# Sums of squares of the new x: their matmuls further back in TensorE's order, their running sum in another tile

## The chip, the core and the metric

The kernel runs on one core of a Trainium2 chip. The metric is the time of one execution on the device in microseconds (us). Engines are named as in the profile: PE is TensorE's matmul side and PEld its weight loads, DVE is VectorE, ACT is ScalarE, POOL is GpSimd, SP is SyncE, whose queue issues most of the DMAs.

## What is computed

Two layers of a decoder trunk are run on 288 tokens: 256 of a prompt and 8 sequences of 4 sample tokens. Each layer has three sub-layers: a SwiGLU feed-forward, a token mixer, and another feed-forward; the mixer of the first layer ("even") is window attention beside an RG-LRU branch, that of the second ("odd") is HGRN2. Each sub-layer is wrapped as follows, and the change touches the root mean square of the new x that the next sub-layer takes:

```python
def _rms_norm(x, gain):
    xf = x.astype(jnp.float32)
    inv = lax.rsqrt(jnp.mean(xf * xf, axis=-1, keepdims=True) + EPS)
    return (xf * inv).astype(x.dtype) * gain.astype(x.dtype)
def _pre(x, c, g_pre, ada_w, ada_b):
    mod = jax.nn.silu(c) @ ada_w + ada_b
    shift, scale, gate = jnp.split(mod[:, None, :], 3, axis=-1)
    return _rms_norm(x, g_pre) * (1 + scale) + shift, gate
def _post(x, y, gate, g_post, res_w):
    return x + res_w * (1 + gate) * _rms_norm(y, g_post)
```

## The kernel before

Activations lie feature-major: x is a tile of 128 partitions by 8 blocks by 288 tokens. Six sub-layers are numbered i = 0 to 5; i = 1 is the even mixer, i = 4 the odd one. Each has an input projection (`proj_in`, PSUM tiles `pj`), its own inner work, and an output projection (`proj_out`, tiles `y`), followed in `out_proj` by the norms and by `pre`, which makes the next input `h`. Weights come as f32 (`raw`, 1 MB each, two buffers) and are split by ACT (`whi`) and DVE (`wlo`) into two halves in a matmul format that PE runs faster; one product of a 128x128 weight block is three matmuls, two with `whi` and one with `wlo` ("a step" below). A wide tile `raw` holds two halves of 1024 columns, one for each output block j.

The conditioning products (`ada`, tiles `aw`, 1 MB each, three buffers) are spread over the whole run in chunks of four matmuls (eight matmul records), and when the last chunk of a group is done, `ada_finish` copies the sums with ACT (`asb`), turns them on PE (`adaT`) and forms `mod`, `modA` or `modG` on DVE.

The order on PE and SP is the program's own order. The program writes it with a planner: `clk["t"]` is a modelled PE clock, main work is a generator (`drive`), and side work is a list of generators (`side`). A side generator that yields a number is taken up again that many modelled microseconds later; one that yields nothing, after what it issued is modelled to end. So a yield in a side generator decides how much of the main work stands ahead of the generator's next matmuls in PE's order. ACT, DVE and POOL are ordered by a list scheduler from the program order and its own estimate of when inputs are ready; PE and SP execute strictly in the order written.

`out_proj` needs, for the mean square of the next x, the mean square of the present x (`clk["xw"]`, tile `xw`). That is what `x_stats` makes: four ACT squares of two blocks of x each (tiles `xsq`), three adds, sixteen small matmul records with a constant weight (`xms`), and one DVE op into `xw`. It runs once at the start, where the adds are on DVE, and four times (i = 0 to 3) as a side generator after `pre`, where the adds are on POOL. `xw` is read only at the end of the sub-layer that follows. The tile `yss` (pool `tp`, one buffer, 3 x 288 columns) is `out_proj`'s running sum of squares of y and of the products with x; it is read last by the sums that `late` issues near the end of the output projection. The `xsq` tiles come from the pool `bp` of 27 buffers, which also holds the mixers' tiles.

In the even mixer `done` puts the first four output blocks into padded tiles `xr`; POOL fills the borders of `xr` from the carried state; `gates` makes the width-4 convolution on DVE (one TENSOR_SCALAR and three SCALAR_TENSOR_TENSOR into `xc` for each of four blocks) and two gate products on PE (`rgr`, `rgi`). POOL's queue there also holds the stores `out_k_old` and `out_v_old`, which copy the carried window from `kc` and `vc` to memory.

Of the kernel before, what the change touches and what calls it, by code (L numbers as in the profile page):

```python
# [9 lines left out]
F32 = mybir.dt.float32  # L10
# [7 lines left out]
NT = 288  # L18
# [31 lines left out]
def tile_trunk(ctx: ExitStack, tc: tile.TileContext, I: dict, O: dict):  # L50
    nc = tc.nc
    SY = nc.sync
    clk = {"t": 0.0, "dma": 0.0, "step": 0.0}
# [82 lines left out]
    tp = ctx.enter_context(tc.tile_pool(name="tp", bufs=8))  # L136
# [3 lines left out]
    def flat(name, dt=F32):  # L140
        return bp.tile([128, 2 * PW], dt, tag="b", name=name)
# [7 lines left out]
    def small(name, shape, tag=None, bufs=None):  # L149
        return sp.tile(shape, F32, tag=tag or "s%d" % int(np.prod(shape[1:])), name=name, bufs=bufs)  # L150

    def aux_ps(name):
        return ps.tile([128, 512], F32, tag="ps", name=name, bufs=8)
# [66 lines left out]
    def after(r, prior):  # L220
        tc.add_manual_dep(r.ins, prior.ins.name, NOSYNC, reason="order")
        return r
# [210 lines left out]
    def mod_of(i):  # L433
        if i not in mods:
            mods[i] = (mp.tile([128, 24, 9], F32, tag="mod", name=f"mod{i}", bufs=3),
                       mp.tile([128, 8, 9], F32, tag="modA", name=f"modA{i}", bufs=3),
                       mp.tile([128, 8, 9], F32, tag="modG", name=f"modG{i}", bufs=3))
        return mods[i]
# [10 lines left out]
    def ada_finish(i, g, acc):  # L449
        mod, mA, mG = mod_of(i)  # L450
        if clk["t"] < clk.get("hold", 0.0):
            yield clk["hold"] - clk["t"] + 0.01
        asb = flat("asb")[:, :512]
        A.activation(asb, acc, AF.Copy)
        yield [asb]
        pt = aux_ps("adaT")
        o, nj = (16, 2) if g else (0, 4)
        for b in range(4):
            if g:
                T.matmul(pt[:, 18 * b:18 * b + 18], lhsT=asb[:, 128 * b:128 * b + 128], rhs=foldg, start=True, stop=True)  # L460
            else:
                T.transpose(pt[:, 128 * b:128 * (b + 1)], asb[:, 128 * b:128 * (b + 1)], ident)
        m = 9 if g else 32
        V.tensor_tensor(
            out=mod[:, o:o + 4 * nj, :].rearrange("p (j b) m -> p b j m", b=4),
            in0=pt[:, :4 * nj * m].rearrange("p (b j m) -> p b j m", b=4, j=nj)[:, :, :, 0:9],
            in1=adab[:, 24 * i + o:24 * i + o + 4 * nj].rearrange("p (j b) -> p b j", b=4).unsqueeze(3)
            .to_broadcast([128, 4, nj, 9]),
            op=OP.add)
        V.scalar_tensor_tensor(out=mG if g else mA, in0=mod[:, 8 + 8 * g:16 + 8 * g, :], scalar=1.0,  # L470
                               in1=(gph if g else gpre)[:, 8 * i:8 * i + 8].unsqueeze(2).to_broadcast([128, 8, 9]),
                               op0=OP.add, op1=OP.mult)
# [20 lines left out]
    def ada_steps(parts):  # L493
        n = ada_st["n"]
        ada_st["n"] += 1
        i, c = chunks[n]
        ada_load_to(n)
        g = int(c >= NC0)
        if c in (0, NC0):
            ada_st["acc"] = aux_ps(f"ada{i}{g}")  # L500
        acc = ada_st["acc"]
        w = aw[n][0]
        m = 512 // parts
        for q in range(parts):
            if q:
                yield
            for j in range(4):
                k = 2 * (c - NC0) + j // 2 if g else c
                T.matmul(acc[32 * j:32 * j + 32, m * q:m * q + m], lhsT=sc[:, k, :],
                         rhs=w[:, 512 * j + m * q:512 * j + m * q + m],  # L510
                         start=c in (0, NC0) and q == 0, stop=c in (NC0 - 1, NCH - 1) and q == parts - 1)
        ada_load_to(n + AW)
        if c in (NC0 - 1, NCH - 1):
            side(ada_finish(i, g, acc))
# [42 lines left out]
    def sums(out, t, first, last, m=None):  # L557
        for j in range(4):
            T.matmul(out[32 * j:32 * j + 32, :], lhsT=mean1 if m is None else m, rhs=t[:, NG * j:NG * j + NG],
                     start=first, stop=last)  # L560
# [24 lines left out]
    def x_stats(prior=None):  # L585
        w = small("xw", [128, NG], tag="xw", bufs=2)
        clk["xw"] = w
        if prior:
            yield 12.0
        t0 = flat("xsq")[:, :2 * NT]  # L590
        for b in range(0, NB, 2):
            t = flat("xsq")[:, :2 * NT] if b else t0
            r = A.activation(t, x[:, b:b + 2, :].rearrange("p c t -> p (c t)"), AF.Square)
            if prior:
                after(r, prior)
            if b:
                (G if prior else V).tensor_tensor(out=t0, in0=t0, in1=t, op=OP.add)
        yield
        p = aux_ps("xms")[:, :NG]
        for c in range(2):  # L600
            sums(p, t0[:, NT * c:NT * c + NT], c == 0, c == 1)
        V.tensor_scalar(out=w, in0=p, scalar1=EPS, scalar2=None, op0=OP.add)
# [103 lines left out]
    def pre_first():  # L706
# [47 lines left out]
        def before(k):  # L754
            if k == 0:
                for _ in x_stats():
                    pass
                ada(0)
                warm(WARM[1])
                u = root(clk["xw"], None, "xiv")  # L760
                refine(u, clk["xw"], V)
                iv = tp.tile([128, NT], F32, tag="ivs", name="ivf", bufs=1)
                A.activation(iv, spread(u, "xivb", 99.0), AF.Copy)
                st["iv"] = iv
                table(AF.Silu)
                finish(0)
                warm(WARM[2])
                ada(1)
                warm(WARM[3])
                finish(1)  # L770
                warm(WARM[4])
            if k + 2 < NB:
                ada(k + 2)
# [19 lines left out]
    def out_proj(i, nk, hk):  # L793
# [120 lines left out]
        if i < NSUB - 2:  # L914
            side(x_stats(da.last))
# [728 lines left out]
```

## Time and profile before

| | us |
|---|---|
| three runs | 1319.61, 1322.71, 1323.49; median 1322.71 |
| the profiled execution | 1321.75 |
| its span, first to last instruction | 1320.0 |
| PE busy | 1281.6 (97%) |
| PEld / DVE / ACT / POOL busy | 1184.9 / 777.1 / 638.2 / 194.2 |
| mean granted TensorE clock | 0.989 of 2.4 GHz |

A row of the timeline gives start, duration, engine, line, operation, the tile written and the tiles read, the number of instructions merged into the row and, in square brackets, the idle time ahead of it with what ended that. The line is that of a helper everywhere, so tiles name the work. In the row of a matmul the start is what counts; ends are modelled. A row of the stretches gives from:to, length, and then the busy time of PE, PEld, DVE, ACT and POOL with instruction counts, the granted clock, the share of the DMA engines' time and GB/s.

### The profile page before, as it was taken

Reading aid. Unit: us, or ns where it says so; the run is one execution under the profiler, and the core shown is the slowest. Engines: PE = TensorE matmul, PEld = TensorE weight load, DVE = VectorE, ACT = ScalarE, POOL = GpSimd, SP = SyncE. Lnnn points to the kernel's source line nnn. Section 1 sums busy time; section 2 is a strip of 40 time slices with the busy share of each in tenths; the row PEclk is TensorE's granted clock in tenths of the full one; section 3 lists DMA queues with packets and bytes.
Section 4 is the critical chain, followed back from the end, with each engine's and each line's share of the span. In section 5 each row is a group of like instructions: output and inputs, shape, how many; then the busy total and the mean of one; then the engine's idle time right before and its main releaser. Section 6 shows DMA issues by size and latency. Waiting matters only on the chain.

```text
span 1320.0 us, 25241 instructions
## 1 busy us (share of the span) xinstructions
PE 1281.6 (97%) x10413; PEld 1184.9 (90%) x10413; DVE 777.1 (59%) x1406; ACT 638.2 (48%) x1091; POOL 194.2 (15%) x295
## 2 busy tenths in 40 slices
PE   9999999969899999999999999999999998999997
PEld 8999999957687899999799999978888988999997
DVE  6635436557846554555555555559788877555442
ACT  5434435456745544444544444464443566444442
POOL 0000001153022100011200001135344131000010
PEclk9999999989989999999999999999999999999999
DMA  9776555396256655444586454467644352555441
GB/s 366 264 313 246 203 211 205 133 373 236 96 212 236 266 205 169 159 160 160 224 323 219 160 164 171 146 263 264 228 157 164 132 192 68 192 174 174 160 160 37
DMA packets 39413, 263.48 MB, mean 200 GB/s; under 512 B 4917, under 2 KB 5493, under 8 KB 9217
## 3 DMA queue, kind: packets, MB, share of 16 engines
q1 hardware_dynamic: 35136, 249.09, 51.7%
q0 software_dynamic: 4160, 12.77, 2.8%
q8 instruction: 82, 1.34, 0.4%
q14 instruction: 35, 0.28, 0.1%
HBM read 254.69 MB, written 7.15 MB: 198 GB/s over the span
## 4 chain that ended last, share of the span: by engine, by line
PE 85%; DVE 6%; ACT 3%; DMA 2%; POOL 2%; issue 1%; DVEq 0%; POOLq 0%; ACTq 0%
PE pj L94 49%; PE y L94 24%; PE ada L94 4%; DVE wlo L94 2%; PE lv L94 1%; DMA aw<-in_w_ada 1%; PE o L94 1%; DMA kc<-in_kc 1%; PE adaT L94 1%; ACT L94 1%; POOL hv L94 1%; DMA raw<-in_wo_in 1%; PE adaf L94 1%; PE warm L94 1%; ACT whi L94 1%
## 5 line engine op out<-in xcount | busy, mean ns | idle before, releaser
L94 PE MATMUL pj<-h,whi 128*128 128x288 f32 x3552 | 723.3, 298 | 1.9 <-ACT h L94 1.8
L94 PEld LDWEIGHTS pj<-h,whi 128*128 128x128 f32 x3552 | 569.3, 188 | 35.3 <-issue 23.1
L94 DVE TENSOR_TENSOR wlo<-raw,whi 128x1024 fp32r<-128x1024 f32 x326 | 400.6, 1240 | 290.2 <-ACT whi L94 288.6
L94 PE MATMUL pj<-h,wlo 128*128 128x288 f32 x1776 | 518.2, 294 | 1.2 <-DVE wlo L94 1.2
L94 ACT ACTIVATE whi<-raw 128x1024 fp32r<-128x1024 f32 x326 | 340.4, 1057 | 350.4 <-PE pj L94 143.1
L94 PEld LDWEIGHTS pj<-h,wlo 128*128 128x128 f32 x1776 | 335.3, 189 | 2.0 <-DVE wlo L94 1.9
L94 PE MATMUL y<-mh,whi 128*128 128x288 f32 x1408 | 280.9, 295 | 0.0
L94 PEld LDWEIGHTS y<-mh,whi 128*128 128x128 f32 x1408 | 225.8, 188 | 2.1 <-issue 1.7
L94 PE MATMUL y<-mh,wlo 128*128 128x288 f32 x704 | 207.9, 295 | 0.0
L94 POOL TENSOR_TENSOR yss<-yss,ysq 128x288 f32<-128x288 f32 x55 | 59.2, 1078 | 798.5 <-ACT ysq L94 790.5
L94 PEld LDWEIGHTS y<-mh,wlo 128*128 128x128 f32 x704 | 132.4, 188 | 0.0
L94 DVE TENSOR_TENSOR fs<-fs,pj 128x288 f32<-128x288 f32 x88 | 39.5, 453 | 93.1 <-PE pj L94 92.1
L94 PE MATMUL ada<-aw,cT 128*32 128x256 f32 (+1 forms) x712 | 71.2, 499 | 3.8 <-DMA aw<-in_w_ada 3.8
L94 ACT ACTIVATE mh<-fs 128x288 fp32r<-128x288 f32 x88 | 37.8, 434 | 58.5 <-DVE fs L94 58.5
L94 ACT ACTIVATE fs<-pj 128x288 f32<-128x288 f32 x88 | 34.8, 400 | 37.2 <-PE pj L94 37.0
L94 DVE TENSOR_TENSOR mh<-fs,mh 128x288 fp32r<-128x288 f32 x88 | 39.5, 453 | 10.7 <-ACT mh L94 10.7
L94 PE MATMUL y<-o,whi 128*128 128x288 f32 x192 | 39.6, 300 | 0.0
L94 ACT ACTIVATE ysq<-y 128x288 f32<-128x288 f32 x42 | 17.0, 405 | 45.1 <-PE y L94 45.1
L94 PEld LDWEIGHTS ada<-aw,cT 128*32 128x32 f32 x712 | 17.2, 110 | 22.2 <-issue 15.5
L94 ACT ACT_TABLE_LOAD x27 | 34.6, 1283 | 5.0 <-DVE oivw L94 3.9
L94 ACT ACTIVATE h<-hv,mod,modA 128x256 fp32r<-128x256 f32 x40 | 23.7, 592 | 21.4 <-DVE hv L94 21.4
L94 DVE TENSOR_TENSOR yg<-y,modG 128x32 f32<-128x32 f32 x48 | 8.9, 186 | 41.6 <-ACT yg L94 41.6
(292 smaller groups left out, 1096.5 us busy)
## 6 DMA issues: line engine op xcount, KB each, us to landing
raw<-in_wf_in SPq DMA_DIRECT2D x88, 1024.0 KB, 5.0
aw<-in_w_ada SPq DMA_DIRECT2D x64, 1024.0 KB, 6.4
raw<-in_wf_out SPq DMA_DIRECT2D x44, 1024.0 KB, 4.9
raw<-in_wo_in SPq DMA_DIRECT2D x16, 1024.0 KB, 7.4
awf<-in_w_ada SPq DMA_DIRECT2D x8, 1024.0 KB, 9.5
raw<-in_we_in SPq DMA_DIRECT2D x7, 1024.0 KB, 7.7
raw<-in_we_out SPq DMA_DIRECT2D x4, 1024.0 KB, 7.1
S<-in_s POOLq DMA_DIRECT2D x16, 256.0 KB, 6.6
```

The costliest lines, as they stand in the source:

```text
L94: r = f(*args, **kw)
```

## The change

Three edits. In `x_stats` the running sum `t0` of the squares no longer takes a tile of `bp` but the first 576 columns of a tile with the tag `yss`. Where `x_stats` runs as a side generator, it now yields 40 modelled microseconds between the adds and the matmuls, where it yielded until the adds were modelled to end. In `ada_finish`, a generator that starts before the end of `pre` (`clk["hold"]`) waits for 3.0 modelled microseconds after that end instead of 0.01. The number of instructions on each engine is the same.

```diff
@@ -449,7 +449,7 @@
     def ada_finish(i, g, acc):
         mod, mA, mG = mod_of(i)
         if clk["t"] < clk.get("hold", 0.0):
-            yield clk["hold"] - clk["t"] + 0.01
+            yield clk["hold"] - clk["t"] + 3.0
         asb = flat("asb")[:, :512]
         A.activation(asb, acc, AF.Copy)
         yield [asb]
@@ -587,7 +587,8 @@
         clk["xw"] = w
         if prior:
             yield 12.0
-        t0 = flat("xsq")[:, :2 * NT]
+        acc = tp.tile([128, 3, NT], F32, tag="yss", name="xss", bufs=1)
+        t0 = acc.rearrange("p c t -> p (c t)")[:, :2 * NT]
         for b in range(0, NB, 2):
             t = flat("xsq")[:, :2 * NT] if b else t0
             r = A.activation(t, x[:, b:b + 2, :].rearrange("p c t -> p (c t)"), AF.Square)
@@ -595,7 +596,7 @@
                 after(r, prior)
             if b:
                 (G if prior else V).tensor_tensor(out=t0, in0=t0, in1=t, op=OP.add)
-        yield
+        yield 40.0 if prior else None
         p = aux_ps("xms")[:, :NG]
         for c in range(2):
             sums(p, t0[:, NT * c:NT * c + NT], c == 0, c == 1)
```

## Rows read from the trace of the kernel before

**Rows 1.** The page's head: the span of the profiled execution.

```profile
span 1320.0 us, 25241 instructions
```

**Rows 2.** PE's waits: waiter, releaser, total us, times, longest us.

```profile
PE xms L94 <- POOL xsq L94: 9.9, 2, 9.4
...
PE adaT L94 <- ACT asb L94: 0.6, 1, 0.6
```

**Rows 3.** Timeline of the even mixer's start: PE around the sums.

```profile
285.39 0.29 PE L94 MATMUL pj<-h,wlo 128*128 128x288 f32 x1
...
295.07 0.71 PE L94 MATMUL xms<-xsq,mean 128*32 128x72 f32 x16 [9.39 <-POOL xsq L94]
```

**Rows 4.** Stretches of 5 us around it: busy us by engine, granted clock, DMA.

```profile
285.00:290.00 5.00, 0.68 (x6) 0.44 (x4) 1.51 (x3) 1.32 (x6) 2.17 (x4) 0.67 1.02 405
290.00:295.00 5.00, 0.00 (x0) 0.00 (x0) 4.09 (x3) 1.74 (x2) 5.00 (x18) 0.50 1.01 360
295.00:300.00 5.00, 4.93 (x33) 2.82 (x33) 4.51 (x10) 0.00 (x0) 0.55 (x3) 0.50 0.49 201
300.00:305.00 5.00, 5.00 (x36) 3.79 (x33) 5.00 (x9) 2.33 (x4) 0.00 (x0) 0.96 0.77 269
```

**Rows 5.** Timeline there, POOL alone.

```profile
288.61 0.55 POOL L1040 DMA_DIRECT2D out_v_old<-vc  x1 [1.27 <-DMA vc<-in_vc]
289.18 1.41 POOL L94 TENSOR_TENSOR xsq<-xsq 128x576 f32<-128x576 f32 x1
...
290.56 0.22 POOL L94 COPY xr<-cin 128x24 f32<-128x24 f32 x1
...
293.64 1.38 POOL L94 TENSOR_TENSOR xsq<-xsq 128x576 f32<-128x576 f32 x1
```

**Rows 6.** Timeline there, DVE alone: the convolution around `xw`.

```profile
293.24 2.13 DVE L94 SCALAR_TENSOR_TENSOR xc<-xr,sm,xc 128x312 f32<-128x312 f32 x1
295.85 0.23 DVE L94 TENSOR_SCALAR xw<-xms 128x72 f32<-128x72 f32 x1 [0.49 <-PE xms L94]
296.00 1.90 DVE L94 SCALAR_TENSOR_TENSOR xc<-xr,sm,xc 128x312 f32<-128x312 f32 x4
...
304.66 0.53 DVE L94 SCALAR_TENSOR_TENSOR xc<-xr,sm,xc 128x312 f32<-128x312 f32 x1
```

**Rows 7.** Timeline there, PE behind the sums: two steps, gate products, a chunk.

```profile
303.06 0.42 PE L94 MATMUL pj<-h,whi 128*128 128x288 f32 x2
...
303.45 0.43 PE L94 MATMUL pj<-h,whi 128*128 128x288 f32 x2
...
304.26 0.69 PE L94 MATMUL rgr<-xc,rgw 128*128 128x312 f32 x2
...
307.23 0.69 PE L94 MATMUL rgr<-xc,rgw 128*128 128x312 f32 x2
...
308.28 0.69 PE L94 MATMUL rgr<-xc,rgw 128*128 128x312 f32 x2
...
309.42 1.06 PE L94 MATMUL ada<-aw,cT 128*32 128x512 f32 x8
```

**Rows 8.** Timeline at the other places: i = 2's start, then the odd mixer's.

```profile
434.98 0.66 PE L94 MATMUL adaT<-ident,asb 128*128 128x128 f32 x4 [0.65 <-ACT asb L94]
...
890.48 0.46 PE L94 MATMUL xms<-xsq,mean 128*32 128x72 f32 x16 [0.47 <-POOL xsq L94]
...
891.07 2.01 ACT L94 ACTIVATE whi<-raw 128x1024 fp32r<-128x1024 f32 x2 [1.29 <-DMA raw<-in_wo_in]
...
891.81 0.78 POOL L94 TENSOR_SCALAR K<-F 128x288 f32<-128x288 f32 x1
...
892.57 1.57 PE L94 MATMUL dg<-Q,K 128*128 128x128 f32 x11
```

**Rows 9.** Timeline of the even mixer's middle: a small product and its DVE reader.

```profile
329.05 0.75 PE L94 MATMUL rp<-rx,rot 128*128 128x288 f32 x2
...
333.61 0.45 DVE L94 TENSOR_TENSOR rx<-rp,cs 128x288 f32<-128x288 f32 x1
```

## The prediction

> **What bounds the kernel now.** I read the page first. PE is busy for 1281.6 of the 1320.0 us of the span [rows 1] and the chain of work that ended last is mostly PE, so only what shortens PE's idle time, or speeds up PE, can show. PE's waits come next: over the whole run it waits 9.9 us for the sums `xms`, in two places, and 9.4 of that in one of them; the other waits are small, among them 0.6 us of `adaT` for its copy `asb` [rows 2]. So the change can gain where the 9.4 us lie, at the start of the even mixer: PE ends a step at 285.39 + 0.29 = 285.68 and starts the sums at 295.07 [rows 3]. The stretches show the second cost: the granted clock falls to 0.50, the lower of its two levels (1.2 GHz), while PE stands, and stays there after PE is back; the mean over 300 to 305 is 0.96, so the higher level returns at about 300.4 (0.4 us of 5 at half) [rows 4].
>
> Then I ask why the sums were late. ACT's squares are early; POOL's adds are late because POOL issues four stores of the carried window first, each held by the load of its tile; the last is issued at 288.61, the first add starts at 289.18 and the last ends at 293.64 + 1.38 = 295.02 [rows 5]. Between these adds, in the same queue, stand the copies that fill the borders of `xr` (290.56) [rows 5]. That is the point of the case: the same late POOL queue also feeds DVE's convolution, and the convolution feeds PE's gate products, which stand 9 us further on in PE's order [rows 7]. What ends last once the sums are gone is DVE.
>
> **The change part by part.** *The wait in the even mixer.* With the sums moved 40 planned us back, PE goes on at 285.68 with what stood between them and the first gate product: about ten steps and two chunks. A step takes 303.45 - 303.06 = 0.39 us and a chunk 1.06 [rows 7], so some 6.0 us; with the eight transposes `adaT`, moved 3 us back, about 1 us more, PE is at the first gate product at 292.7. It cannot run it then. DVE's row of the convolution at 293.24 ends at 295.37; then `xw` waited 0.49 and took 0.23, and the next four operations ran from 296.00 to 297.90 [rows 6]. The first block of `xc` is among those. Without `xw` they start at 295.37, 0.63 us earlier, and so does everything behind them on DVE, which was busy in all of 300 to 305 and in 4.51 us of the 5 before [rows 4]. The last operation of the fourth block ended at 304.66 + 0.53 = 305.19 [rows 6] and will end at 304.56. PE's fourth pair of gate products then starts 0.05 us later (the lag from POOL's add to the sums, 295.02 to 295.07 [rows 3, 5]) and takes 309.42 - 308.28 = 1.14 us [rows 7]: the chunk behind it starts at 305.75 where it started at 309.42. So of 9.4 us of wait at most 3.7 come back here; the rest is waited for by `rgr` instead of `xms`.
>
> The clock takes part of it. PE will idle from 292.7 to about 297.3 and then in short pieces; idle from 285.68 on, it was at the lower level in all of 290 to 295 [rows 4]. If it is low at the fourth pair, that pair takes 2.28 us and ends at 306.9: 2.5 us are left. Before, the level came back 5.3 us after PE had resumed (295.07 to 300.4) [rows 3, 4]; counted from the third pair, now near 303, that is 308.3, and the 1.4 us to there lose half of it, 0.7. So the ends are 1.8 us (low throughout) and 3.7 us (full throughout). No row is nearer to one of them, PE being busy for about a quarter of 292.7 to 304 (two pairs, a small product and a step); I take the middle, 2.7.
>
> The Trainium skill ("TensorE: Matmul & The Clock Gate", section "Part 1: The HAM clock gate") says that TensorE left idle goes back to half rate and is given the full rate again only after sustained work. That speaks against this change, because it leaves an idle gap in the same place; by the rule the term would be the low end, 1.8, and by a clock that only a gap as long as the old one lowers it would be 3.7. The 0.50 at 290 to 300 agrees with the rule for the long gap; no row shows a gap of 4 to 5 us broken by short work.
>
> *The sums in their new place.* Sixteen records cost 0.46 us at full clock [rows 8]. In the even mixer they stood in a stretch that DVE will bound, so their old place gives nothing back and the new place costs 0.46, above 0 and below 0.7 (the half-clock row [rows 3]). That leaves 2.2 us for the mixer. In the feed-forwards the work is moved from one dense stretch to another: 0.
>
> *i = 2's start.* The sums did not wait there; `adaT` behind them waits 0.65 us for its copy [rows 8]. That generator starts after `hold`, so it is not moved. PE comes 0.46 us earlier; the copy does not. Bounds: -0.46 (all waited away) to +0.65 (the planner puts other steps in front); I take 0, the planner's clock being 0.5 us early there too. *The odd mixer.* 0.47 us of wait and 0.46 of sums leave this place [rows 8]. But the next side product, `dg`, needs K, whose second half POOL ends at 891.81 + 0.78 = 892.59, while `dg` starts at 892.57 and lasts 1.57 for both halves [rows 8]; PE can't be more than some tenths earlier there. Bounds 0 to 0.9; I take 0.2. *i = 3's start* has no wait [rows 2]: 0.
>
> *The 3 us in `ada_finish`.* It acts at the two mixers, where the generator starts before `hold`. Queued behind the copy `asb` on ACT are the splits `whi`; if the list scheduler puts the copy behind two splits that wait for their weights (891.07 to 893.08 in the odd mixer [rows 8]), PE's transposes wait for it. In the even mixer the wait of PE for the convolution hides that; in the odd mixer it costs up to 2.6 us. I take 0, since the copy's place in the program stays ahead of those splits, and keep -2.6.
>
> *The tile.* `yss` is last read by the sums near 257 and next written after the mixer's own output products, so it adds no wait; `bp` has one tile less in use. SP: the loads of the next `aw` tiles, queued behind chunks, go out up to 11 us earlier, into stretches whose DMA engines are full (1.02, 1.01) [rows 4]; what they could delay, the weights of output blocks 8 and 9, is needed only behind the fourth gate pair. 0.
>
> Sum: 2.7 - 0.46 + 0 + 0.2 = 2.4 us. The profiled execution took 1321.75, so 1319.35; the median of the three runs is 0.96 above it, so the forecast is 1322.71 - 2.4 = 1320.3, its own range 1317.4 (3.7 + 0.65 + 0.9 = 5.3 gained) to 1322.2 (0.5 gained).
>
> **The rivals.** *A, the wait comes back in full.* It needs DVE's convolution not to be the next bound: the list scheduler draws up DVE's and POOL's orders anew and could put the border copies ahead of the adds. For it: the largest wait in the profile, and the lower clock behind it. Against it: the copies stand behind the same four stores and DVE's queue was full from 295.9 on [rows 4 to 6]. Gain: 9.39, plus half of the 4.93 us that PE ran at 0.50 (2.47) [rows 4], plus 0.65 and 0.47 [rows 8]: 13.0, so 1309.7; a part of it gives 5 to 13. *B, nothing is left.* The 2.4 us are lost again in the mixer's second half, where DVE carries the softmax; 1322.7, give or take 1. For it: DVE's lag there; against it: all of that follows PE's output blocks in order. *C, slower.* The sums' new place lies near 328 in the even mixer, where DVE lags: `rp` started on PE at 329.05 and its reader on DVE at 333.61, 4.6 us later [rows 9]. `xw` joins that queue and holds one of the eight PSUM banks meanwhile. If PE's next output tile needs that bank, PE stands for up to 4.6 us and runs as long at the lower level behind it as it did before, 2.47: 1322.7 - 2.4 + 4.6 + 2.5 = 1327.4. It decides from the point where all other seven banks are in use within the 4.6 us. That the sums aren't moved at all is no rival: PE's order is written out by the program.
>
> **How the numbers follow.** Forecast 0.48, A (whole or in part) 0.23, B 0.19, C 0.10. 0.3% is 4.0 us, about what a measurement of this kernel can tell from no change. Faster by more: all of A and a fifth of the forecast, 0.33; slower by more: C, 0.10; the rest, 0.57, within. A alone holds more than the 0.2 that may be left out, so the range goes from 1309.5 to 1324.5 and leaves out C and the tails.
>
> **What would show it.** Right: in the changed trace `xms` waits nowhere, PE's longest wait at the even mixer's start is `rgr` for `xc`, of 4 to 6 us, the granted clock still touches 0.50 between 290 and 305, and the chunk behind the fourth gate pair starts at 305.5 to 307.5. Wrong: no PE wait over 2 us there (A); the same chunk earlier but the output projection of the mixer no earlier than 374 (B); a wait of a `pj` tile near 328 with `xw` as its releaser (C); `adaT` waiting for `asb` in the odd mixer (the 2.6 us).

## The result and the profile after

The changed kernel is slower.

| | before | after |
|---|---|---|
| median of four executions each, us | 1321.45 (1319.61 to 1323.49) | 1332.47 (1331.56 to 1334.03) |
| ratio after to before | | 1.0084, 95% interval 1.0064 to 1.0105 |
| profiled execution / its span | 1321.75 / 1320.0 | 1331.56 / 1329.8 |
| mean granted TensorE clock | 0.989 | 0.988 |

The forecast was 1320.3 with a range of 1309.5 to 1324.5, and slower by over 0.3% had the smallest chance, 0.10. The head of the page of the changed kernel answers [rows 1]:

```profile
span 1329.8 us, 25239 instructions
```

The section on the change has the number of instructions on each engine the same. On PE it is not: the pages count 10407 where the kernel before has 10413; DVE, ACT and POOL have as many as before. That is a first sign of a program drawn up anew.

The waits of PE over the whole run (waiter, releaser, total us, times, longest us) answer [rows 2]:

```profile
PE pv L94 <- ACT pTs L94: 5.7, 3, 4.1
PE rgr L94 <- issue: 5.2, 1, 5.2
PE rgr L94 <- DVE xc L94: 3.8, 2, 3.6
...
PE pT L94 <- DVE den L94: 2.2, 1, 2.2
PE adaT L94 <- ACT asb L94: 2.0, 3, 1.4
```

The 9.4 us of `xms` for POOL are gone, as the change wants. In their place PE waits for the gate products `rgr` (9.0 us together; the first of these waits has no releaser in the profile, but stands ahead of the first product that needs `xc`) and, further on, in the attention (`pv`, `pT`). PE around the gates, against [rows 3, 7]: the last step, the four `rgr`, and the chunk behind them.

```profile
292.34 0.29 PE L94 MATMUL pj<-h,wlo 128*128 128x288 f32 x1
297.79 1.38 PE L94 MATMUL rgr<-xc,rgw 128*128 128x312 f32 x2 [5.16 <-issue]
...
300.01 1.38 PE L94 MATMUL rgr<-xc,rgw 128*128 128x312 f32 x2
...
302.64 1.38 PE L94 MATMUL rgr<-xc,rgw 128*128 128x312 f32 x2 [0.22 <-DVE xc L94]
...
308.17 1.38 PE L94 MATMUL rgr<-xc,rgw 128*128 128x312 f32 x2 [3.62 <-DVE xc L94]
...
310.52 1.94 PE L94 MATMUL ada<-aw,cT 128*32 128x512 f32 x8
```

The first gate product is near where the prediction put it (297.3), the chunk behind the fourth pair 1.1 us later than before instead of 1.8 to 3.7 earlier, and nothing but gate products stands between 292.6 and 310.5. The stretches (columns as in [rows 4]) show the clock. It is still 1.00 in 290 to 295, goes to the lower level (0.50 in the stretches of 1 us) while PE waits for the first gate, and again around the fourth pair; it was 1.00 from 305 on in the kernel before (the last row).

```profile
290.00:295.00 5.00, 2.63 (x22) 2.40 (x18) 2.96 (x3) 2.00 (x2) 4.98 (x18) 1.00 1.03 399
295.00:300.00 5.00, 2.21 (x4) 1.20 (x5) 5.00 (x11) 2.82 (x4) 1.69 (x3) 0.71 1.02 425
300.00:305.00 5.00, 4.33 (x9) 2.22 (x8) 5.00 (x7) 2.50 (x5) 2.93 (x2) 0.61 0.51 213
305.00:310.00 5.00, 1.83 (x4) 1.18 (x4) 4.16 (x6) 0.52 (x2) 1.68 (x1) 0.73 0.00 0
310.00:315.00 5.00, 5.00 (x22) 2.58 (x21) 0.58 (x2) 4.39 (x8) 0.96 (x2) 0.59 0.31 72
```

```profile
305.00:310.00 5.00, 5.00 (x27) 3.21 (x25) 3.15 (x5) 4.10 (x8) 2.96 (x3) 1.00 0.37 154
```

The decisive view is none of these but the order of PE's instructions in the two programs. From `adaT` of the even mixer on (a step is one accumulating step of an output block):

```
before   adaT, 2 steps, SUMS, 3 steps, chunk, 3 steps, chunk, 4 steps,
         pair 0, pair 1, rp, 1 step, pair 2, pair 3, chunk, 7 steps, ...
changed  chunk, adaT, 3 steps, chunk, 6 steps,
         pair 0, pair 1, pair 2, pair 3, chunk, 1 step, rp, 9 steps, ...
```

Not only the sums have moved. The program draws up PE's order by a clock of its own while it issues instructions; without the sums (0.56 us on that clock) and with the later transposes, side work falls due at other steps. All four gate pairs come together, three steps earlier, and the attention's products come out in another order too. The prediction took for granted that the rest of the order only shifts. The order on ACT, DVE and POOL is drawn up from the program's order, so it can change as well; the attention below shows it on ACT.

How much each stretch lost I worked out from the stretches of 1 us: idle is the length less PE's busy time, half-clock loss is the busy time times one less the granted clock. Both together, in the even mixer: 12.1 us before and 16.3 after in 285 to 318, 0.8 and 1.9 in 318 to 345, 10.2 and 12.0 in 345 to 400. From 256 to 400 that is 24.5 and 31.8. From the end of i = 0 to the end of i = 1 (both at the product `xivb`) before took 147.67 us and the changed kernel 154.98, 7.3 more:

```profile
262.68 1.11 PE L94 MATMUL xivb<-xiv,pick 128*128 128x72 f32 x8
410.35 1.11 PE L94 MATMUL xivb<-xiv,pick 128*128 128x72 f32 x8
```

and in the changed kernel

```profile
263.26 1.11 PE L94 MATMUL xivb<-xiv,pick 128*128 128x72 f32 x8
418.24 1.11 PE L94 MATMUL xivb<-xiv,pick 128*128 128x72 f32 x8 [1.02 <-DVE xiv L94]
```

Over the whole of i = 1 the lost time is 26.9 and 35.1, 8.2 apart, so it accounts for the longer mixer within about 1 us (within some 2 us in the kernels below). The rest of the 9.8 us of span is 0.6 ahead of 263, 0.3 in i = 2 and 3 together and 1.8 in the odd mixer (222.89 and 224.65, `xivb` to `xivb`), less 0.1 behind it.

### The profile page after: what moved, and what is told of

Read it like the earlier page. It is cut to its first block, busy times and chain, and to the rows that moved or that the text cites. A ratio compares the mean times of both kernels' runs of the same rounds, so it can differ in the third digit from the quotient of the medians.

```text
span 1329.8 us, 25239 instructions
## 1 busy us (share of the span) xinstructions
PE 1286.7 (97%) x10407; PEld 1186.7 (89%) x10407; DVE 780.1 (59%) x1406; ACT 637.9 (48%) x1091; POOL 191.7 (14%) x295
## 4 chain that ended last, share of the span: by engine, by line
PE 61%; DVE 4%; ACT 3%; DMA 2%; issue 1%; POOL 1%; SPq 0%; DVEq 0%; ACTq 0%; POOLq 0%
PE pj L94 36%; PE y L94 17%; PE ada L94 2%; DVE wlo L94 2%; PE lv L94 1%; DMA S<-in_s 1%; PE o L94 1%; POOL hv L94 1%; DMA raw<-in_wo_out 1%; DVE yg L94 1%; ACT hv L94 1%; ACT whi L94 1%; DVE hv L94 0%; ACT L94 0%; DVE x L94 0%
## 5 line engine op out<-in xcount | busy, mean ns | idle before, releaser
L94 DVE TENSOR_TENSOR mh<-fs,mh 128x288 fp32r<-128x288 f32 x88 | 39.5, 452 | 10.2 <-ACT mh L94 10.2
L94 PEld LDWEIGHTS y<-o,whi 128*128 128x128 f32 x192 | 31.5, 192 | 1.9 <-ACT tab L94 0.8
```

Of the source, the lines that this page charges most:

```text
L94: r = f(*args, **kw)
```

## The experiments

Theory 1: the move of the sums is worth what was forecast, and the order drawn up anew costs (in the first kernels narrower: the order at the gates). Rivals: the later transposes hold up DVE's convolution (theory 2), or the sums cost in their new place, whatever the order (theories 3 and 4). Ratios are to the kernel before on the same chip, with 95% intervals; its own executions there lay between 1314.85 and 1327.19, so a difference under some 0.2% is not told apart. Lengths come from the one profiled execution of each kernel: even is the end of i = 0 to the end of i = 1, odd the end of i = 3 to the end of i = 4, and lost the sum of above for the three stretches of the even mixer (the stretches are the same in time, not in work). Two kernels whose even mixers have the same order (before and the fourth row) differ by 2.8 us in that length, so single lengths are read with that in mind. Most of this spread goes with the granted clock: of 33 executions of the kernel before on one chip the fastest took 1315.96 us at a mean clock of 0.993, the slowest 1326.88 at 0.984. A profile shows one execution: that of the pinned sums is 5.3 us faster than their median, those of the change and of the change pinned in the even mixer lie within 1 us of theirs.

| kernel | ratio | even | odd | lost 285-318, 318-345, 345-400 |
|---|---|---|---|---|
| before | 1 | 147.67 | 222.89 | 12.1, 0.8, 10.2 |
| the change | 1.0084 (1.0064 to 1.0105) | 154.98 | 224.65 | 16.3, 1.9, 12.0 |
| sums and tile alone | 1.0119 (1.0072 to 1.0167) | 159.98 | 223.78 | 14.3, 0.3, 18.7 |
| sums moved in the other places only | 0.9989 (0.9965 to 1.0014) | 144.92 | 221.31 | 12.4, 0.9, 7.7 |
| hold alone | 1.0040 (1.0016 to 1.0063) | 144.19 | 226.21 | 12.3, 0.8, 9.8 |
| hold, even mixer alone | 0.9999 (0.9980 to 1.0017) | 143.11 | 223.19 | 13.3, 0.8, 8.1 |
| sums moved, order pinned | 0.9991 (0.9966 to 1.0016) | 142.63 | 222.41 | 9.7, 0.6, 9.2 |
| the change, order pinned | 1.0036 (1.0017 to 1.0054) | 143.74 | 227.57 | 13.3, 0.5, 8.1 |
| the change, pinned in the even mixer | 1.0009 (0.9990 to 1.0027) | 145.16 | 224.99 | 15.1, 0.5, 7.1 |
| order alone, sums in place | 1.0103 (1.0074 to 1.0133) | 150.25 | 230.81 | 11.5, 2.9, 10.7 |
| order alone, even mixer | 1.0072 (1.0044 to 1.0100) | 150.69 | 223.83 | 11.7, 2.4, 11.3 |
| change, gates further back | 1.0083 (1.0057 to 1.0109) | 151.74 | 224.47 | 8.5, 3.4, 14.7 |
| before, stores later | 0.9998 (0.9977 to 1.0020) | 144.48 | 222.65 | 8.8, 0.7, 11.1 |
| change, stores later | 1.0041 (1.0020 to 1.0062) | 148.76 | 225.35 | 6.2, 7.4, 11.0 |
| pinned sums, stores later | 0.9986 (0.9964 to 1.0009) | 142.54 | 227.51 | 6.4, 0.8, 12.4 |
| change, gaps filled | 1.0108 (1.0073 to 1.0142) | 152.27 | 224.57 | 6.1, 2.7, 10.6 |
| pinned sums, gaps filled | 1.0000 (0.9981 to 1.0020) | 147.38 | 223.07 | 5.2, 0.6, 7.0 |

**One part at a time.** The change's two halves alone:

```diff
-            yield clk["hold"] - clk["t"] + 0.01
+            yield clk["hold"] - clk["t"] + 3.0
```

> The kernel before with only the 3.0 us in ada_finish; the sums stay where they were. Its program puts the eight transposes after one more chunk and the gate pairs as two, three steps, two, and the sums stay in front of them. Theory 1 (the loss comes from PE's order: with the sums gone from there, all four gate pairs come together, ahead of the steps of output block 5, so PE stands at them with the steps behind it): the order is little changed, so 1321 to 1324 us, ratio 0.999 to 1.002. Theory 2 (the transposes pushed into the convolution: mod and modG and the splits shift on DVE, so the convolution is late): most of the 10 us, 1328 to 1333. Theory 3 (the sums in their new place disturb the softmax half): nothing, 1321.

The other half is the changed kernel with the 0.01 put back:

> The changed kernel with the 0.01 us in ada_finish as before: the sums and the tile alone. All four gate pairs stand together on PE, with four steps of output block 5 less ahead of them than before. Theory 1 (PE's order at the gates): slower than before, 1327 to 1333, ratio 1.004 to 1.009, a wait of 3 us or more at the first and at the fourth gate pair. Theory 2 (the transposes): about the forecast, 1319 to 1322, ratio 0.998 to 1.000. Theory 3 (the sums in the softmax half): slower by nearly all, 1329 to 1333, the lag arising from 328 us on.

And the sums moved everywhere but in the even mixer:

```diff
-            side(x_stats(da.last))
+            side(x_stats(da.last, 40.0 if i else None))
...
-        yield
+        yield later
```

> The sums moved by 40 planned us at the three later places alone (i = 2 and 3 and the odd mixer), not in the even mixer, and 0.01 in ada_finish. Theory 1 and 3 (all of the loss but some 2 us arises in the even mixer): 1320 to 1324, ratio 0.999 to 1.002, the landmark xivb at the end of i = 1 at 410 to 411 and at the end of the last but one at 1089 to 1092. A rival (the loss of 1.5 to 2 us between 868 and 1100 is the odd mixer's own): xivb of i = 4 at 1091.5 to 1092.

The sums alone are the slow half, 16 us; in the other three places they cost nothing. Theory 2 falls: without the later transposes it is not faster. But the hold cost 0.4% too, more than theory 1 had, and its even mixer is as short as before; its odd mixer is 3.3 us longer. PE's order there is another one, with side products at other steps; PE's longest waits in the odd mixer of that kernel:

```profile
PE vtp L94 <- ACT vs L94: 1.9, 1, 1.9
PE xivb L94 <- DVE xiv L94: 1.7, 1, 1.7
PE adaT L94 <- ACT asb L94: 1.5, 1, 1.5
PE xyms L94 <- DVE ysq L94: 1.1, 1, 1.1
```

The waits are others than before, but hardly more: PE idles for 8.5 us there, for 7.6 before. 3.4 us are half-clock loss, where the profile of before has none and the next kernel, whose odd mixer has the order of before, has 1.6. So the new order as the reason of the longer odd mixer is argued, not shown.

To see whether that is the hold's whole price, it was left out of the odd mixer, whose order is then that of before:

```diff
-            yield clk["hold"] - clk["t"] + 0.01
+            yield clk["hold"] - clk["t"] + (3.0 if i < 3 else 0.01)
```

> The 3.0 us in ada_finish in the even mixer alone, the rest as before; PE's order of the odd mixer is that of the kernel before. If the hold alone cost 0.4% by the odd mixer's new order: 0.997 to 1.001, the odd mixer at 221 to 223 us. Rival (it cost in the even mixer): 1.003 to 1.005.

0.9999: the hold's 0.4% arises in the odd mixer. The prices of the two halves don't add up (0.40% and 1.19%, together 0.84%); with the hold, the sums' move gives yet another order, which fits, though no run tests it.

**The move without the new order.** The program's clock is charged for the sums at their old place and put back behind them at the new one, so that everything else on PE stays in the order of before; only the sums stand elsewhere, in the even mixer behind the second scores (at 334.47). In one kernel with 0.01 and in one with the whole change:

```diff
-        yield 40.0 if prior else None
+        yield
+        if prior:
+            clk["t"] = max(clk["t"], ready(t0)) + 8 * 0.07
+            place("V", clk["t"] + 0.12, 0.07 + NG / 960)
+            clk["step"] = clk["t"] + 0.12 + 0.07 + NG / 960
+            yield 40.0
+        kept, queues = dict(clk), {q: list(v) for q, v in held.items()}
...
         V.tensor_scalar(out=w, in0=p, scalar1=EPS, scalar2=None, op0=OP.add)
+        if prior:
+            clk.update({q: kept[q] for q in ("t", "end", "step")})
+            held.update(queues)
```

> The sums and the tile alone (0.01 us in ada_finish), but the program's own clock is charged for the sums at their old place and not at the new one, so that PE's order of everything else stays that of the kernel before: in the even mixer only the sums stand elsewhere, behind the first scores. That is what the prediction took for granted. Theory 1 (the loss comes from the order that the program draws up anew once its clock lacks the sums): the forecast holds, ratio 0.995 to 1.001, the first gate product near 297.3, the chunk behind the fourth pair at 305.5 to 307.5, PE's lost time (idle, and half of what it runs at the lower clock) between 285 and 318 at 8 to 11 us where before had 12.1. Theory 4 (the sums gone from there and put in the softmax half cost as such, whatever the order): 1.006 to 1.012.

> The whole change, the 3.0 us in ada_finish included, with PE's order pinned as in the pinned sums: the program's clock is charged for the sums at their old place and not at the new one, so the rest of the order is that of the hold alone. Theory 1 (the order drawn up anew is what costs): about the hold alone less some 2 us, ratio 1.001 to 1.005. Rival (the parts cost together whatever the order): 1.006 to 1.010 as the change itself.

PE at the gates in the pinned sums, its four `rgr` and the chunk:

```profile
297.88 1.38 PE L94 MATMUL rgr<-xc,rgw 128*128 128x312 f32 x2 [5.75 <-issue]
...
300.09 1.25 PE L94 MATMUL rgr<-xc,rgw 128*128 128x312 f32 x2
...
304.25 0.79 PE L94 MATMUL rgr<-xc,rgw 128*128 128x312 f32 x2 [0.96 <-DVE xc L94]
...
306.39 0.76 PE L94 MATMUL rgr<-xc,rgw 128*128 128x312 f32 x2 [0.82 <-DVE xc L94]
...
307.60 1.07 PE L94 MATMUL ada<-aw,cT 128*32 128x512 f32 x8
```

and two of its stretches, where the clock is back at 1.00 for all of 305 to 310:

```profile
300.00:305.00 5.00, 4.04 (x13) 2.74 (x12) 5.00 (x8) 2.51 (x4) 1.92 (x2) 0.77 0.55 231
305.00:310.00 5.00, 4.18 (x25) 2.31 (x24) 4.44 (x6) 3.82 (x6) 2.19 (x3) 1.00 0.16 21
```

Here something of the forecast's size is seen: first gate at 297.88, chunk at 307.60 (0.1 us outside the window given), 2.4 us less lost in 285 to 318 where the forecast had 2.2 for the mixer, ratio 0.9991. The interval (0.9966 to 1.0016) holds the forecast of 0.998 and also no change at all. With the hold the pinned change is at 1.0036, as the hold alone. The sums' new place as such costs nothing that can be seen, so theories 3 and 4 fall.

**The new order without the move.** The mirror: the sums stay on PE where they were, and the clock is charged for them 40 us later, in all places or in the even mixer alone (the tile is the change's, the hold 0.01):

```diff
+        kept, queues = dict(clk), {q: list(v) for q, v in held.items()}
         p = aux_ps("xms")[:, :NG]
...
+        if prior:
+            clk.update({q: kept[q] for q in ("t", "end", "step")})
+            held.update(queues)
+            yield 40.0
+            clk["t"] = max(clk["t"], ready(t0)) + 8 * 0.07
+            place("V", clk["t"] + 0.12, 0.07 + NG / 960)
```

> The mirror of the pinned sums: the sums stay on PE where the kernel before has them, but the program's clock is charged for them 40 us later, so that PE's order of the rest is nearly that of the sums alone (all four gate pairs together, two thirds of the attention's order too). Theory 1 (the order costs, not the move): slower, 1.003 to 1.010, with more lost time in the second half of the mixer (345 to 400) than the 10.2 us of before. Rival (the order is harmless, the sums' new place costs): 0.998 to 1.002.

> The order of the even mixer alone: the sums stay on PE where the kernel before has them, and in the even mixer only the program's clock is charged for them 40 us later; PE's order of the odd mixer is that of the kernel before. Theory 1 (the order drawn up anew in the even mixer costs by itself): 1.002 to 1.006, the end of i = 1 (xivb) 2 to 7 us after the one of before, the odd mixer as long as before (221 to 223 us). Rival (in the order-only run it was the odd mixer alone, where 230.8 us stood against 222.9): 0.998 to 1.001.

And the reverse of the second, the whole change with the order pinned in the even mixer alone (the odd mixer keeps the change's order):

> The whole change with PE's order pinned in the even mixer alone; in the odd mixer it is the changed kernel's. Theory 1 (the even mixer's new order is some 6 us of the change's loss, the rest is the odd mixer's): 1.002 to 1.005, the odd mixer at 224 to 226 us. Rival (the even mixer's order is not the cause): 1.007 to 1.010.

The reverse decides. Without its new order in the even mixer the change is at 1.0009, so this order is worth 0.75%, some 10 of the 11 us. The mirror agrees in its direction: the order alone, with the sums in their old place, costs 0.72%. But in that kernel's profile 3.0 us of this are in the mixer, where the change loses 7.3, and 4.0 in i = 2, where the unmoved sums now come too early and wait 2.8 us; the change, which has moved them there too, loses only 0.5 there. Both ratios lie outside the ranges given, the reverse's below and the mirror's above. The first mirror loses 7.9 in the odd mixer as well, so it says more of the odd mixer than of this change.

Against the pinned kernel with everything else equal (the ninth row), the changed kernel loses 1.2 us more at the gates, 1.4 in 318 to 345 and 4.9 in 345 to 400; the last two are the attention; of the 4.9, 3.2 are idle time and 1.7 the lower clock. The largest wait there is that of a product `pv` for the copy `pTs` of the transposes `pT` ahead of it. In the changed kernel two steps lie between them on PE:

```profile
349.68 0.66 PE L94 MATMUL pT<-ident,sm 128*128 128x128 f32 x4
355.24 1.97 PE L94 MATMUL pv<-pTs,vt 128*64 128x256 f32 x4 [4.10 <-ACT pTs L94]
```

and the transposes end at 350.34, but ACT has a split, a copy and eight small operations of the softmax ahead of `pTs` in its queue:

```profile
350.64 1.06 ACT L94 ACTIVATE whi<-raw 128x1024 fp32r<-128x1024 f32 x1 [0.81 <-PE pj L94]
351.60 0.39 ACT L94 ACTIVATE gx<-pj 128x288 f32<-128x288 f32 x1
351.89 0.50 ACT L94 ACTIVATE sm<-sm,mx 128x256 f32<-128x256 f32 x1
...
354.60 0.58 ACT L94 ACTIVATE pTs<-pT 128x512 f32<-128x512 f32 x1
```

The same pair in the pinned sums, with the order of before, has one step and the third scores between, fewer than 2 us of work, and nothing waits:

```profile
338.00 0.63 PE L94 MATMUL pT<-ident,sm 128*128 128x128 f32 x4 [0.56 <-DVE sm L94]
...
340.04 1.08 PE L94 MATMUL pv<-pTs,vt 128*64 128x256 f32 x4
```

because ACT makes the copy at once and the softmax behind it:

```profile
338.67 0.60 ACT L94 ACTIVATE pTs<-pT 128x512 f32<-128x512 f32 x1 [2.35 <-PE pT L94]
339.16 0.50 ACT L94 ACTIVATE sm<-sm,mx 128x256 f32<-128x256 f32 x1
```

In the changed kernel the third scores stand ahead of these transposes on PE, and ACT's order has their softmax ahead of the copy. So the wait comes from the new order on PE and ACT together; no run changes one engine's order alone. In the order-alone kernel (even mixer) the same wait, from 318 to 400, is 8.0 us where the kernel before has 2.8:

```profile
PE pv L94 <- ACT pTs L94: 8.0, 4, 5.5
```

**The gates alone.** In the changed kernel, the gate products 10 planned us further back, so that PE has steps ahead of them:

```diff
-            yield
+            yield 10.0
             pr = aux_ps("rgr")[:, :CW]
```

> The changed kernel with the gate products of each block 10 planned us further back: on PE all eight steps of output block 5 and four of block 6 stand before the first gate pair; DVE's order of the convolution is the one of the changed kernel. Theory 1 (PE's order at the gates): the loss is gone, 1317 to 1323, ratio to the kernel before 0.997 to 1.001; waits at rgr under 2 us together. Theory 2 (DVE's convolution itself later): PE waits for the splits of block 6 or the convolution as long as before, 1328 to 1333. Theory 3 (the sums in the softmax half): the lag of the gates goes, that of the second half stays, 1325 to 1329.

The gates are mended (8.5 us lost there, under the 12.1 of before, first scores at 325.76 where before had 327.99), and the time is as bad as the change's: 14.7 us are lost in 345 to 400, 5.0 idle and 9.7 at the lower clock. The attention's order is new once more; that this is the reason is likely, but not tested by itself. So the gates' place by itself, the narrow form of theory 1, is not the cause; that form fell here.

**The common cause of both late queues.** The prediction put the sums' and the convolution's lateness down to four stores on POOL. They were issued at output block 9 instead:

```diff
-        for c in range(2):
-            G.dma_start(O["k_old"][:, 4 * c:4 * c + 4, :], kcv[c][:, :, TS:])
-            G.dma_start(O["v_old"][:, 4 * c:4 * c + 4, :], vcv[c][TS:])
...
                 if j == 9:
+                    for c in range(2):
+                        G.dma_start(O["k_old"][:, 4 * c:4 * c + 4, :], kcv[c][:, :, TS:])
+                        G.dma_start(O["v_old"][:, 4 * c:4 * c + 4, :], vcv[c][TS:])
                     side(attention())
```

in the kernel before, in the changed one, and in the pinned sums:

> The kernel before with POOL's four stores of the carried window issued at output block 9 instead of before the mixer's first block, PE's order unchanged. If POOL's late queue is what both the sums and the convolution wait for: the sums wait under 3 us, DVE's first operation of the convolution starts at 286.5 to 288.5 instead of 290.81, the first gate product at 295 to 299, lost time in 285 to 318 at 2 to 6 us, ratio 0.992 to 0.997. Rival (the convolution is held by the loads or by DVE's splits anyway, or the stores come to stand in front of something later): 0.998 to 1.003.

> The changed kernel with the four stores at output block 9, PE's order that of the changed kernel. If the gates in a block cost only because the convolution is late: the first gate product starts at 292 to 295, waits at rgr under 3 us together, lost time in 285 to 318 falls from 16.3 to 3 to 8 us; the second half of the mixer keeps its own order, so ratio to the kernel before 0.995 to 1.002. Rival (the gates' place costs by itself): 1.005 to 1.009.

> The sums moved with PE's order pinned, and the four stores at output block 9. If both causes are as said: no wait for the sums and little for the gates, lost time in 285 to 318 at 2 to 5 us, ratio 0.990 to 0.996, not slower than the kernel before with the stores alone. Rival (a bound behind the convolution, such as the splits of the weights): as the pinned sums alone.

The late queue is as said; its price is not. In the pinned sums the convolution starts at 286.11 on DVE (290.81 before) and the first gate product at 293.07, without a wait; the fourth still waits:

```profile
301.59 0.76 PE L94 MATMUL rgr<-xc,rgw 128*128 128x312 f32 x2 [3.17 <-DVE xc L94]
```

What is lost in 285 to 318 falls from 9.7 to 6.4 us in the pinned sums, from 12.1 to 8.8 in the kernel before and from 16.3 to 6.2 in the changed one. The times follow in the changed kernel only (1.0041); in the other two the 3.3 us are not found in them (0.9986 and 0.9998, both intervals reach below 0.998), and all three ratios lie above the ranges given. The profile of the pinned one can't show where they went: it is the slowest of its eleven executions, that of the pinned sums the second fastest of its own. Its odd mixer is 5.1 us longer, and 3.4 of that are the lower clock (5.1 us of half-clock loss for 1.6), 1.7 idle time.

**The clock behind the gaps.** Products that nothing reads, put where PE stood, with the program's clock not charged; 22 and 14 ahead of the first and fourth pair in the changed kernel, 24 ahead of the first pair and 12 ahead of a `pv` in the pinned sums (`FILL` stands for these numbers at the gates):

```diff
+            if b in FILL:
+                t0 = clk["t"]
+                warm(FILL[b])
+                clk["t"] = t0
             pr = aux_ps("rgr")[:, :CW]
```

> The changed kernel with 22 products that nothing reads put on PE ahead of the first gate product and 14 ahead of the fourth pair's, where PE stood idle for 5.16 and 3.62 us; the program's clock isn't charged for them. If the lower clock behind these gaps is a cost of its own: the granted clock stays at 1.00 through 295 to 315, half-clock loss in 285 to 318 falls from 5.9 to under 1.5 us, ratio to the kernel before 1.003 to 1.006. Rival (the clock is given back later, PE being bound by DVE there): 1.007 to 1.010.

> The pinned sums with 24 products that nothing reads ahead of the first gate product (where PE stood idle for 5.7 us) and 12 ahead of the product that waits for pTs near 357 (2.76 us). If the lower clock behind the two gaps costs: half-clock loss 2.2 us in 285 to 318 falls under 0.7, and that of 345 to 400 from 3.4 under 1.5; ratio to the kernel before 0.993 to 0.998, faster than both kernels. Rival: as the pinned sums, 0.997 to 1.001.

In the changed kernel the clock does stay up where the gaps were:

```profile
295.00:300.00 5.00, 5.00 (x38) 4.39 (x37) 5.00 (x12) 3.24 (x5) 1.15 (x3) 1.00 1.01 421
300.00:305.00 5.00, 3.60 (x23) 2.83 (x22) 5.00 (x6) 2.18 (x5) 3.45 (x3) 1.00 0.44 180
305.00:310.00 5.00, 3.11 (x22) 2.16 (x24) 3.63 (x5) 0.79 (x2) 0.14 (x1) 1.00 0.00 0
```

Its half-clock loss in 285 to 318 is 1.7 us instead of 5.9 and its even mixer 2.7 us shorter, but its time is no better (1.0108); in its profile i = 2 and 3 are 2.4 us longer. The clock won there did not show at the end. The pinned sums gain nothing either (1.0000), but there no clock was won: PE now waits 3.19 us at the third pair,

```profile
304.15 1.36 PE L94 MATMUL rgr<-xc,rgw 128*128 128x312 f32 x2 [3.19 <-DVE xc L94]
```

half-clock loss is 1.6 us for 2.2 in 285 to 318, and 5.1 for 3.4 in 345 to 400. So this run doesn't tell what the clock is worth. (In these two rows of the table the filling counts as busy.) Both expectations were wrong. None of the kernels here beats the kernel before by more than can be told.

## Why the prediction was wrong, point by point

**What bounds the kernel; where the wait goes.** Right. The wait of `xms` is gone, PE waits 5.16 us at the first gate product, at 297.79 for a forecast of 297.3, and DVE's convolution, held by the same late POOL queue, is next; the later stores show it. That PE comes to the gate at 292.63, for a forecast of 292.7, is luck: three steps are missing there and `adaT` waits 1.42 us for its copy. Of the four signs of being right only the last, the chunk's start, failed; the first three tell of the move and not of the order.

**The step that failed** stands in three places of the prediction: PE goes on "with what stood between" the sums and the gates, in the second half "all of that follows PE's output blocks in order" (against rival B), and "PE's order is written out by the program". That last is true, and is why the step fails: the program writes it by its own clock, the edit changes that clock, and side work is put where it falls due by it. With the order pinned, the sums' move is at 0.9991, where the forecast fits within what can be told; drawn up anew, the order costs 0.75% in the even mixer, by waits such as that of `pv` for a copy that ACT's order now has late. The diff shows two numbers and a tile; what they do to the order is seen only in the program's listing, and its clock knows little of what happens here: by it the first gate product comes 8.0 us behind the start of the eight transposes before and 8.5 after, where the traces have 20.6 and 11.1.

**The end of the convolution.** Forecast for the last operation of the fourth block: 304.56. In the changed kernel:

```profile
301.38 1.12 DVE L94 SCALAR_TENSOR_TENSOR xc<-xr,sm,xc 128x312 f32<-128x312 f32 x1
...
303.91 1.12 DVE L94 SCALAR_TENSOR_TENSOR xc<-xr,sm,xc 128x312 f32<-128x312 f32 x1
...
306.08 1.12 DVE L94 SCALAR_TENSOR_TENSOR xc<-xr,sm,xc 128x312 f32<-128x312 f32 x1
...
307.49 0.53 DVE L94 SCALAR_TENSOR_TENSOR xc<-xr,sm,xc 128x312 f32<-128x312 f32 x1
```

It ends at 308.02, 3.5 us late. POOL's last store is issued at 289.72 instead of 288.61, which is 1.1; `mod` and `modG` of the later transposes now lie between (0.3), so does the first product of `kv` (0.4), and three operations take 1.12 us where the fourth takes 0.53 (last section), which is 1.8. In the pinned sums it ends at 306.24, 1.7 late:

```profile
305.71 0.53 DVE L94 SCALAR_TENSOR_TENSOR xc<-xr,sm,xc 128x312 f32<-128x312 f32 x1
```

I counted what leaves DVE's queue (`xw`), and not what an earlier first gate lets loose on POOL.

**The clock's part of the term.** Forecast: the chunk 1.8 us earlier with the lower level throughout, 3.7 with the higher, the middle taken. Pinned it came 1.8 earlier, but not by the clock: that was back at 1.00 from 303 on, the fourth pair took 1.21 us, and it was the convolution that ended late. That it falls on the low end is luck. In the changed order a second gap, 3.62 us ahead of the fourth pair, brought the lower level again until 314, and the half-clock loss is 5.9 us.

**The sums' 0.46 us and `xw`.** Right: `xms` took 0.46 us in its new place in the even mixer of the pinned sums (334.47, where the prediction had it near 328), and no product waited for `xw`; rival C did not happen. The slower side had its 0.10 for a mechanism that is not there, and the one that is there had no chance of its own.

**i = 2 and 3.** Forecast 0; 0.3 together.

**The odd mixer and the hold.** Forecast 0.2 gained, bound -2.6 should `adaT` wait behind the splits. It lost 1.8 in the changed kernel, 1.7 of it half-clock loss; its PE idles no longer there than before (7.4 and 7.6 us). The hold alone cost 0.4%, in the odd mixer, so a term put at 0 was worth some 5 us by itself; `adaT` waits only 1.5 us there. The sign of the bound was right; the mechanism stays open, the order being one candidate and the clock another.

**The range.** It ended at 1324.5 because every term was taken from the order of before. The bounds were those of known waits; the order was taken as known and had no bound.

## What to carry to other kernels

Where a program places instructions by a clock of its own, an edit to one of them is an edit to the order of all that come after. Compare the two programs' orders, on the bounding engine and on those that feed it, before any wait is priced; and to learn what the move itself is worth, pin that clock and measure the move and the new order each alone. A wait that a row shows is the price of one order, not of the instruction that happens to stand there.

## What the runs showed of the hardware

Three of DVE's operations of the convolution, each with two tensor inputs, took longer where POOL multiplied at the same time. POOL in the changed kernel:

```profile
300.85 1.31 POOL L94 TENSOR_TENSOR ii<-ii,xc 128x312 f32<-128x312 f32 x1 [4.16 <-ACT ii L94]
303.06 1.62 POOL L94 TENSOR_TENSOR ii<-ii,xc 128x312 f32<-128x312 f32 x1 [0.90 <-ACT ii L94]
305.18 1.68 POOL L94 TENSOR_TENSOR ii<-ii,xc 128x312 f32<-128x312 f32 x1 [0.50 <-ACT ii L94]
```

These lie across the three operations of 1.12 us above; the same operation takes 0.53 with POOL idle, and POOL's third and fourth products take 0.85 in the kernel before, where they come after the convolution. A split `wlo` that began ahead of POOL's product kept its 1.21 us (302.77 in the changed kernel), one that began behind it took 1.86 (306.53 in the pinned sums, the product at 306.20). The convolution's groups by form (count | total us, mean ns, idle before) say the same; before:

```profile
L94 DVE SCALAR_TENSOR_TENSOR xc<-xr,sm,xc 128x312 f32<-128x312 f32 x12 | 7.5, 666 | 0.0
```

and after:

```profile
L94 DVE SCALAR_TENSOR_TENSOR xc<-xr,sm,xc 128x312 f32<-128x312 f32 x12 | 9.4, 809 | 0.0
```

The Trainium skill ("GPSIMD Engine Reference", section "1. Specifications") says that GpSimd shares its SBUF interfaces with VectorE and contends with its instructions that have two SBUF inputs; these rows agree, 0.59 us on each.

The clock did not follow the length of the gap alone. In the kernel before PE stood from 285.68, and the clock was at 0.50 from 287 on; in the changed kernel PE stood from 292.63, and the clock was at 1.00 until 297 and at 0.50 from there to 303. A gap of 3.62 us, ahead of which the gate products had run mostly at the lower level, had it low until 314; one of 1.51 us, in the changed kernel with filled gaps, was followed by 0.50 from 287 to 290; gaps of 0.96 and 0.82 us in the pinned sums left it at 1.00.
